# SSD mixer of a two-layer diffusion backbone: both directions' decay factors from one masked exponent tile

## The chip, the core and the metric

The kernel runs on one core of a Trainium2 chip. TensorE (PE) multiplies matrices, VectorE (DVE) and ScalarE (ACT) do element-wise work, GpSimd (POOL) a smaller share of it, and SyncE's queue (SP) issues the DMAs. Each engine works through its own instructions in order and waits for the others by semaphores. The metric is the device time of one execution in microseconds.

## The reference, cut to what matters

Two layers act on 256 latent tokens and 256 context tokens of width 1024, float32 throughout. A layer is a SwiGLU half step, a token mixer and another SwiGLU half step. Layer 0's mixer is a bidirectional Mamba-2 SSD with 32 heads of 64 channels in 4 groups, state 128, and chunks of 128 tokens; layer 1's is a pooling mixer. The change lies in the SSD, in the part of a chunk that stays within the chunk:

```python
seg = a_cum[:, :, :, None] - a_cum[:, :, None, :]
mask = jnp.tril(jnp.ones((Q, Q), dtype=bool))[:, :, None, None]
Lmat = jnp.exp(jnp.where(mask, seg, -jnp.inf))
cb = jnp.einsum('bclgn,bcsgn->bclsg', Cc, Bc)
y_diag = jnp.einsum('bclsg,bclsge,bcsgep->bclgep', cb, Lmat, xdt)
...
y_lat = d_skip[:, None] * xl
for d in range(2):                       # d == 1 runs on flipped sequences
    ...
    y_lat = y_lat + flip(yl, d)
```

For a pair of tokens (s, t) the forward direction counts where s is not behind t, the backward direction where s is not ahead of t. The two meet only on the diagonal s = t, where the exponent is zero and the factor is the step dt of each direction. `d_skip` multiplies the token itself and is added once.

## The kernel before

The program is a straight line of instructions. A scheduler orders each engine's instructions from the program order by its own estimate of readiness, and semaphores are placed after that. So a change of the code in one place can move rows on every engine.

The first feed-forward part ends at about 404 us of the span, the mixer fills the time from its first projection at 412 us to about 713 us, and the other feed-forward parts and the pooling mixer follow. In the feed-forward parts and the projections each float32 weight tile arrives by DMA (`raw`), ACT rounds it to `hi` (L203), DVE, or POOL for some tiles, takes the rest `lo` (L208), and TensorE makes three products (L216 to L218). The weight tiles of the mixer live in a pool of four buffers.

The mixer works group by group, g = 0 to 3, eight heads each. The string `PLAN` sets the program order of its steps, one letter each: A projects and convolves (`ip`, `ca`, `xs`, and the transposes `ptr`), E makes the decay factors (`decays`), D multiplies them with the matrix C·B (`decays_cb`), Z makes the gate (`pz`), B makes the outputs (`stage_b`) and O the out-projection (`op`).

In E a DMA spreads one row of cumulated exponents per head over 128 partitions, into a tile `em` of 128 x 2048 per direction (L700). There are two `em` buffers in all, one for each direction. For even heads DVE clamps and shifts the exponents (L710) and ACT takes the exponential (L717). For odd heads ACT does the clamp as a Relu (L715) and the exponential (L719). In D TensorE forms C·B for both chunks (`pcb`), DVE masks it with one triangle per direction (L734), multiplies both directions' tiles by it (L742), and POOL adds the two (L743).

In B the states are made: DVE weights x (`x2`, L777 and L783), TensorE multiplies (`ph` L778, `p1` L785), ACT copies `h0` (L780), POOL scales it into `h1` (L787), and DVE adds `p1` to it (L788). POOL multiplies the token by the skip (L799), TensorE applies the summed factors (`py` L803) and the states (`po` L807). DVE adds the parts, and the gate, the norm and the transposes `pyt` (L833) end the group.

The two PSUM banks of tag "b" serve `ptr`, `pcb` and `pyt` here. POOL cannot run L787 before what stands ahead of it in its own order, and DVE not L777 of the second direction before L788 of the first.

Of the kernel before, what the change touches and what calls it, by code (L numbers as in the profile page):

```python
# [20 lines left out]
S = 256  # L21
NG = 4
HG = 8
# [13 lines left out]
C_DSK = C_ALOG + 64  # L37
# [29 lines left out]
def tile_hybrid_backbone(  # L67
# [19 lines left out]
    nc = tc.nc  # L87
    v, sc, pe, gp = nc.vector, nc.scalar, nc.tensor, nc.gpsimd
# [5 lines left out]
    small = ctx.enter_context(tc.tile_pool(name="small", bufs=4))  # L94
# [193 lines left out]
    ONE = slice(0, S)  # L288
# [301 lines left out]
    with ExitStack() as st:  # L590
        scp = st.enter_context(tc.tile_pool(name="scp", bufs=1))
# [53 lines left out]
        def bc8(ap):  # L645
            return ap.unsqueeze(2).to_broadcast([P, HG, HD])

        def h8(ap):
            return ap.rearrange("p (h x) -> p h x", x=HD)
# [43 lines left out]


        def decays(g, EM):
            for d in range(2):
                h0 = 32 * d + HG * g
                em = sd.tile([P, HG, 2, P], F32, tag="em", name="em")
                src = acd[h0 : h0 + HG, :].rearrange("h t -> (h t)").unsqueeze(0).to_broadcast([P, HG * S])
                nc.sync.dma_start(em.rearrange("p h j t -> p (h j t)"), src)  # L700
                EM.append(em)
            yield
            for d in range(2):
                for h in range(HG):
                    e = EM[d][:, h]
                    hc = 32 * d + HG * g + h

                    for j in range(2):
                        if h % 2 == 0:
                            v.tensor_scalar(  # L710
                                e[:, j, :], e[:, j, :], ac[:, 2 + j, hc : hc + 1], qs[:, j, hc : hc + 1],
                                op0=ALU.min, op1=ALU.add,
                            )
                        else:
                            sc.activation(e[:, j, :], e[:, j, :], AF.Relu, scale=-1.0, bias=ac[:, 2 + j, hc : hc + 1])  # L715
                    if h % 2:
                        sc.activation(EM[d][:, h - 1], EM[d][:, h - 1], AF.Exp)  # L717
                        for j in range(2):
                            sc.activation(e[:, j, :], e[:, j, :], AF.Exp, scale=-1.0, bias=ld[:, j, hc : hc + 1])  # L719
                        yield  # L720

        def decays_cb(g, A, EM):
            BT, CT = A["BT"], A["CT"]
            pcb = bank("pcb", "b")
            for j in range(2):
                pe.matmul(
                    pcb[:, j * P : (j + 1) * P], BT[:, S + j * P : S + (j + 1) * P], CT[:, j * P : (j + 1) * P],
                    start=True, stop=True,
                )
            cbs = []  # L730
            for d in range(2):
                cbm = XH[d][:, ONE].rearrange("p (j t) -> p j t", t=P)
                cbs.append(cbm)
                v.tensor_tensor(  # L734
                    cbm, pcb[:, 0:S].rearrange("p (j t) -> p j t", t=P),
                    tri[d].unsqueeze(1).to_broadcast([P, 2, P]), op=ALU.mult,
                )
            for j in range(2):
                for d in range(2):
                    cbm = cbs[d]  # L740
                    e = EM[d][:, :, j, :]
                    v.tensor_tensor(e, e, cbm[:, j, :].unsqueeze(1).to_broadcast([P, HG, P]), op=ALU.mult)  # L742
                gp.tensor_tensor(EM[0][:, :, j, :], EM[0][:, :, j, :], EM[1][:, :, j, :], op=ALU.add)  # L743
            yield


# [22 lines left out]
        def stage_b(g, A, EM, zs):  # L769
            CT, Bt, xt = A["CT"], A["Bt"], A["xt"]  # L770
            hin = []
            for d in range(2):
# [8 lines left out]
                j = 2 + d  # L781
# [14 lines left out]
            for j in range(2):  # L796
                xl = xt[:, 2 + j, :]
                y = sd.tile([P, 512], F32, tag="y", name="y")
                gp.tensor_tensor(h8(y), h8(xl), bc8(pk[:, C_DSK + HG * g : C_DSK + HG * g + HG]), op=ALU.mult)  # L799
                py = bank("py", "c")  # L800
                for h in range(HG):
                    hc = slice(h * HD, (h + 1) * HD)
                    pe.matmul(py[:, hc], EM[0][:, h, j, :], xl[:, hc], start=True, stop=True)  # L803
                v.tensor_tensor(y, y, py, op=ALU.add)
                for d in range(2):
                    po = bank("po", "c")
# [120 lines left out]
            v.tensor_tensor(w2[:, j, c], w2[:, j, c], to[:, k, c], op=ALU.add)  # L927
        sc.activation(w2, w2, AF.Exp)
        v.tensor_tensor(w2, w2, dtk, op=ALU.mult)
        eL = scp.tile([P, 64], F32, name="eL")  # L930
        for d in range(2):
            c = slice(32 * d, 32 * d + 32)
# [178 lines left out]
def _layout(inputs):  # L1111
# [32 lines left out]
    for g, w in enumerate((2, 4, 8, 16)):  # L1144
        def box(n):
# [11 lines left out]
            for l in range(2)  # L1157
# [11 lines left out]
    return {  # L1169
        "hx": np.concatenate([a["ctx"][0], a["x"][0]]),  # L1170
        "hxT": np.concatenate([a["ctx"][0].T, a["x"][0].T], axis=1),
                "pack": pack, "idn": np.eye(P, dtype=f), "tris": tris, "pmat": pmat, "gnorm": a["ssd_norm_g"].reshape(1, 2048),
        "ada": ada, "adan": adan, "wgu": wgu, "wd": wd, "win": win, "wz": wz,
        "wout": wout, "poolw": pw,
    }
# [20 lines left out]
```

## Time and profile before

| quantity | value |
|---|---|
| median of 3 runs | 1315.9 us (1314.4 to 1316.13) |
| profiled execution, its own time | 1308.84 us |
| span of that execution | 1307.1 us |
| PE busy over the span | 1248.1 us (95%) |
| DVE busy | 972.6 us (74%) |
| ACT busy | 596.7 us (46%) |
| POOL busy | 157.9 us (12%) |
| mean granted TensorE clock | 0.984 |

The profiled execution's own time is 1.7 us above its span. Shares over the whole span mix stages, so the views below are taken of the mixer, from 446 us (the end of the preparation of its exponents) to 713 us (the start of the last out-projection). In a timeline row the first number is the start, the second the time of the row's instructions together, and the brackets hold the engine's idle time before it and what released it.

### The profile page before, as it was taken

Reading aid. Unit: us, or ns where it says so; the run is one execution under the profiler, and the core shown is the slowest. Engines: PE = TensorE matmul, PEld = TensorE weight load, DVE = VectorE, ACT = ScalarE, POOL = GpSimd, SP = SyncE. Lnnn points to the kernel's source line nnn. Section 1 sums busy time; section 2 is a strip of 40 time slices with the busy share of each in tenths; the row PEclk is TensorE's granted clock in tenths of the full one; section 3 lists DMA queues with packets and bytes.
Section 4 is the critical chain, followed back from the end, with each engine's and each line's share of the span. In section 5 each row is a group of like instructions: output and inputs, shape, how many; then the busy total and the mean of one; then the engine's idle time right before and its main releaser. Section 6 shows DMA issues by size and latency. Waiting matters only on the chain.

```text
span 1307.1 us, 21106 instructions
## 1 busy us (share of the span) xinstructions
PE 1248.1 (95%) x8262; PEld 1110.3 (85%) x8262; DVE 972.6 (74%) x1545; ACT 596.7 (46%) x1023; POOL 157.9 (12%) x112
## 2 busy tenths in 40 slices
PE   5999999999999979999988999999999999999997
PEld 2688888888888757787776999999999999999997
DVE  3599988763367879988997998766978566965553
ACT  3342222222244766555453654544545446744441
POOL 1000000000003242434263300000200000200000
PEclk7999999999999989999999999999999999999999
DMA  9588888962223513434343599767689665375661
GB/s 351 185 312 278 270 314 310 312 226 86 76 93 105 176 52 123 160 115 146 134 148 118 194 326 323 263 207 243 240 311 314 184 207 189 106 240 194 181 184 33
DMA packets 74995, 262.45 MB, mean 201 GB/s; under 512 B 8272, under 2 KB 10768, under 8 KB 73872
## 3 DMA queue, kind: packets, MB, share of 16 engines
q1 hardware_dynamic: 74896, 261.11, 59.1%
q8 instruction: 65, 1.06, 0.3%
q14 instruction: 34, 0.28, 0.1%
HBM read 259.96 MB, written 1.11 MB: 200 GB/s over the span
## 4 chain that ended last, share of the span: by engine, by line
PE 76%; DVE 9%; DMA 5%; ACT 4%; issue 3%; POOL 3%; SPq 0%; POOLq 0%; DVEq 0%; ACTq 0%
PE gu L218 14%; PE gu L216 14%; PE gu L217 14%; PE dn L216 7%; PE dn L218 7%; PE dn L217 7%; DMA adaw<-in_ada_dram 4%; DVE lo L208 2%; DVE ca L630 1%; POOL em L743 1%; PE ip L218 1%; PE ip L217 1%; PE ip L216 1%; PE py L803 1%; PE po L807 1%
## 5 line engine op out<-in xcount | busy, mean ns | idle before, releaser
L208 DVE TENSOR_TENSOR lo<-raw,hi 128x1024 fp32r<-128x1024 f32 (+1 forms) x317 | 393.3, 1244 | 145.9 <-ACT hi L203 145.3
L203 ACT ACTIVATE hi<-raw 128x1024 fp32r<-128x1024 f32 (+1 forms) x333 | 342.0, 1037 | 299.9 <-PE dn L218 125.8
L216 PE MATMUL gu<-vh,hi 128*128 128x256 f32 (+1 forms) x1056 | 293.3, 278 | 4.5 <-DVE sg L1002 2.6
L218 PE MATMUL gu<-vl,hi 128*128 128x256 f32 (+1 forms) x1056 | 292.5, 277 | 0.2 <-DVE vl L991 0.2
L217 PE MATMUL gu<-vh,lo 128*128 128x256 f32 (+1 forms) x1056 | 292.6, 277 | 0.0
L145 DVE SCALAR_TENSOR_TENSOR junk<-adaw,cb 128x1024 bf16<-128x1024 f32 x152 | 183.9, 1222 | 43.9 <-DMA adaw<-in_ada_dram 43.2
L216 PE MATMUL dn<-hh,hi 128*128 128x256 f32 (+1 forms) x704 | 214.2, 304 | 0.0
L217 PE MATMUL dn<-hh,lo 128*128 128x256 f32 (+1 forms) x704 | 214.2, 304 | 0.0
L218 PE MATMUL dn<-hl,hi 128*128 128x256 f32 (+1 forms) x704 | 214.2, 304 | 0.0
L216 PEld LDWEIGHTS gu<-vh,hi 128*128 128x128 f32 x1056 | 198.7, 188 | 5.2 <-DVE sg L1002 2.8
L218 PEld LDWEIGHTS gu<-vl,hi 128*128 128x128 f32 x1056 | 198.4, 188 | 0.5 <-DVE vl L991 0.4
L217 PEld LDWEIGHTS gu<-vh,lo 128*128 128x128 f32 x1056 | 198.6, 188 | 0.0
L218 PEld LDWEIGHTS dn<-hl,hi 128*128 128x128 f32 x704 | 132.1, 188 | 6.9
L217 PEld LDWEIGHTS dn<-hh,lo 128*128 128x128 f32 x704 | 132.1, 188 | 6.9
L216 PE MATMUL gu<-uh,hi 128*128 128x512 f32 x352 | 138.0, 392 | 0.0
L216 PEld LDWEIGHTS dn<-hh,hi 128*128 128x128 f32 x704 | 132.1, 188 | 6.8
L218 PE MATMUL gu<-ul,hi 128*128 128x512 f32 x352 | 137.9, 392 | 0.0
L217 PE MATMUL gu<-uh,lo 128*128 128x512 f32 x352 | 137.4, 390 | 0.0
L257 POOL TENSOR_TENSOR rs<-ms,mhalf 128x2 f32<-128x2 f32 (+1 forms) x6 | 5.4, 906 | 934.4 <-DVE ms L255 934.4
L307 ACT ACTIVATE hh<-hf 128x256 fp32r<-128x256 f32 (+1 forms) x88 | 40.9, 465 | 91.5 <-DVE hf L338 90.0
L336 ACT ACTIVATE sg<-gu 128x256 f32<-128x256 f32 (+1 forms) x79 | 34.7, 439 | 98.2 <-PE gu L218 98.2
L218 PEld LDWEIGHTS gu<-ul,hi 128*128 128x128 f32 x352 | 66.2, 188 | 15.2 <-issue 0.8
(264 smaller groups left out, 1883.6 us busy)
## 6 DMA issues: line engine op xcount, KB each, us to landing
raw<-in_wgu_dram SPq DMA_DIRECT2D x176, 512.0 KB, 4.6
adaw<-in_ada_dram SPq DMA_DIRECT2D x128, 512.0 KB, 5.0
raw<-in_wd_dram SPq DMA_DIRECT2D x64, 512.0 KB, 3.7
raw<-in_win_dram SPq DMA_DIRECT2D x25, 512.0 KB, 3.4
raw<-in_wd_dram SPq DMA_DIRECT2D x32, 384.0 KB, 3.6
adan<-in_adan_dram SPq DMA_DIRECT2D x16, 512.0 KB, 8.4
raw<-in_wz_dram SPq DMA_DIRECT2D x16, 512.0 KB, 3.7
em<-acd SPq DMA_DIRECT2D x8, 1024.0 KB, 4.8
```

What stands on the lines that cost most here:

```text
L145: v.scalar_tensor_tensor(junk, w, 1.0, cb2[i], op0=ALU.mult, op1=ALU.mult, accum_out=M[l][:, t, i : i + 1])
L203: sc.activation(hi[:, 0:n], r[:, 0:n], AF.Copy)
L208: (sub or v).tensor_tensor(lo[:, 0:n], r[:, 0:n], f32(hi[:, 0:n]), op=ALU.subtract)
L216: pe.matmul(out, wh, xh, start=start, stop=False)
L217: pe.matmul(out, wl, xh, start=False, stop=False)
L218: pe.matmul(out, wh, xl, start=False, stop=stop)
L307: sc.activation(a, h, AF.Copy)
L336: sc.activation(sg, pg, AF.Silu)
L630: v.scalar_tensor_tensor(avw[:, :, lo:hi], ov[:, :, lo + off : hi + off], hw[:, 5 * t + k : 5 * t + k + 1], avw[:, :, lo:hi], op0=ALU.mult ...
L743: gp.tensor_tensor(EM[0][:, :, j, :], EM[0][:, :, j, :], EM[1][:, :, j, :], op=ALU.add)
L803: pe.matmul(py[:, hc], EM[0][:, h, j, :], xl[:, hc], start=True, stop=True)
L807: pe.matmul(po, CT[:, j * P : (j + 1) * P], hin[d][0 if j == d else 1], start=True, stop=True)
```

## The change

Both directions now share one exponent tile. E loads the backward exponents first (`back`), then the forward ones (`e`). ACT shifts the backward ones by the difference `qd` of the two directions' per-token terms, as 16 Identity activations with a bias. A TensorE transpose of a strictly upper triangle (`above`) puts the mask for s behind t into a PSUM bank of tag "b" (`pmk`). DVE copies the masked backward exponents into the forward tile with two predicated copies. ACT then takes the exponential of that one tile with the forward bias, 16 activations of 128 x 128. The clamps go away, since no masked-out place is raised to a power any more.

In D, ACT copies C·B out of PSUM once. DVE multiplies the one tile by it, two instructions of 128 x 1024 where there were four, and POOL's sum is gone. The diagonal of the one tile carries the forward share only, so DVE reads the diagonal of C·B with an accumulating instruction and forms `co` = dt(backward) · diagonal + skip. L799's product takes `co` in place of the skip. `qd` and `above` are made once.

```diff
         def decays(g, EM):
-            for d in range(2):
-                h0 = 32 * d + HG * g
+            for d in (1, 0):
                 em = sd.tile([P, HG, 2, P], F32, tag="em", name="em")
...
+            back, e = EM
             yield
-                        if h % 2 == 0:
-                            v.tensor_scalar(
-                                e[:, j, :], e[:, j, :], ac[:, 2 + j, hc : hc + 1], qs[:, j, hc : hc + 1],
-                                op0=ALU.min, op1=ALU.add,
-                            )
-                        else:
-                            sc.activation(e[:, j, :], e[:, j, :], AF.Relu, scale=-1.0, bias=ac[:, 2 + j, hc : hc + 1])
-                    if h % 2:
-                        sc.activation(EM[d][:, h - 1], EM[d][:, h - 1], AF.Exp)
-                        for j in range(2):
-                            sc.activation(e[:, j, :], e[:, j, :], AF.Exp, scale=-1.0, bias=ld[:, j, hc : hc + 1])
-                        yield
+            for h in range(HG):
+                for j in range(2):
+                    sc.activation(
+                        back[:, h, j, :], back[:, h, j, :], AF.Identity, bias=qd[:, j, hcs[h] : hcs[h] + 1]
+                    )
+                if h % 2 and h < HG - 1:
+                    yield
+            pm = bank("pmk", "b")
+            pe.transpose(pm[:, 0:P], above, ident)
+            below = pm[:, 0:P].bitcast(mybir.dt.int32).unsqueeze(1).to_broadcast([P, HG, P])
+            for j in range(2):
+                v.copy_predicated(e[:, :, j, :], below, back[:, :, j, :])
+            yield
+            for h in range(HG):
+                for j in range(2):
+                    sc.activation(e[:, h, j, :], e[:, h, j, :], AF.Exp, bias=qs[:, j, hcs[h] : hcs[h] + 1])
+                if h % 2:
+                    yield
...
-            for d in range(2):
-                cbm = XH[d][:, ONE].rearrange("p (j t) -> p j t", t=P)
...
+            cb = XH[0][:, ONE]
+            sc.activation(cb, pcb[:, 0:S], AF.Copy)
...
-                gp.tensor_tensor(EM[0][:, :, j, :], EM[0][:, :, j, :], EM[1][:, :, j, :], op=ALU.add)
+                v.scalar_tensor_tensor(
+                    tmp("jd", "a", P), cj, 1.0, ident, op0=ALU.mult, op1=ALU.mult, accum_out=dg[:, j : j + 1]
+                )
+                v.scalar_tensor_tensor(
+                    co[:, j, :], dtk[:, 2 + j, 32 + HG * g : 32 + HG * g + HG], dg[:, j : j + 1],
+                    pk[:, C_DSK + HG * g : C_DSK + HG * g + HG], op0=ALU.mult, op1=ALU.add,
+                )
+                e = EM[1][:, :, j, :]
+                v.tensor_tensor(e, e, cj.unsqueeze(1).to_broadcast([P, HG, P]), op=ALU.mult)
...
-                gp.tensor_tensor(h8(y), h8(xl), bc8(pk[:, C_DSK + HG * g : C_DSK + HG * g + HG]), op=ALU.mult)
+                gp.tensor_tensor(h8(y), h8(xl), bc8(A["co"][:, j, :]), op=ALU.mult)
```

The change moves rows as well. On PE, at the first group's states and factors, before (`uh` and `ul` are the tokens, `x` under `ph` the weighted tokens `x2`):

```order
L755 MATMUL pz<-hi,uh_3282 128x512 x2
L642 MATMUL ptr<-cs,xs 128x128 x4
L778 MATMUL ph<-x_3877,Bt 128x512
L778 MATMUL ph<-x_3880,Bt 128x512
L785 MATMUL p_3887<-x_3885,Bt 128x512
L778 MATMUL ph<-x_3893,Bt 128x512
L778 MATMUL ph<-x_3896,Bt 128x512
L785 MATMUL p_3903<-x_3901,Bt 128x512
L803 MATMUL py<-xt,em 128x64 x8
```

and after:

```order
L783 MATMUL ph<-x_3864,Bt 128x512
L783 MATMUL ph<-x_3867,Bt 128x512
L218 MATMUL ip<-ul_3295,hi 128x512
L790 MATMUL p_3874<-x_3872,Bt 128x512
L216 MATMUL ip<-uh_3288,hi 128x512
L217 MATMUL ip<-uh_3288,lo 128x512
L783 MATMUL ph<-x_3880,Bt 128x512
L783 MATMUL ph<-x_3883,Bt 128x512
L218 MATMUL ip<-ul_3296,hi 128x512
L216 MATMUL ip<-uh_3289,hi 128x512
L217 MATMUL ip<-uh_3289,lo 128x512
L790 MATMUL p_3890<-x_3888,Bt 128x512
```

Before, the six state products stood in one block right after a transpose. Now 16 more projection products of the mixer stand ahead of them, and six stand between them.

On DVE, at the end of the second group's outputs, where the third group's factors are made, before:

```order
L804 TENSOR_TENSOR y<-y,py 128x512
L810 TENSOR_TENSOR yo<-po,ea 128x512
L821 TENSOR_SCALAR rs_4682<-rs_4680 128x1
L208 TENSOR_TENSOR lo<-raw,hi 128x1024
L824 SCALAR_TENSOR_TENSOR y<-y,rs_4682,x_85 128x256
L824 SCALAR_TENSOR_TENSOR y<-y,rs_4682,x_86 128x256
L811 TENSOR_TENSOR y<-y,yo 128x512
L810 TENSOR_TENSOR yo<-po,ea 128x512
L710 TENSOR_SCALAR em<-em,ac,qs 128x128 x4
```

and after:

```order
L809 TENSOR_TENSOR y<-y,py 128x512
L829 SCALAR_TENSOR_TENSOR y<-y,rs_4643,x_85 128x256
L829 SCALAR_TENSOR_TENSOR y<-y,rs_4643,x_86 128x256
L815 TENSOR_TENSOR yo<-po,ea 128x512 x2
L816 TENSOR_TENSOR y<-y,yo 128x512 x2
L716 COPY_PREDICATED em<-pmk,em 128x8x128 x2
L826 TENSOR_SCALAR rs_4727<-rs_4725 128x1
L829 SCALAR_TENSOR_TENSOR y<-y,rs_4727,x_85 128x256
L829 SCALAR_TENSOR_TENSOR y<-y,rs_4727,x_86 128x256
```

The two predicated copies, which read both tiles of exponents, now stand six instructions behind the last use of `py` (the `x2` rows count twice); the tile of forward exponents that they read is loaded into the buffer that this `py` has just released.

## Rows read from the trace of the kernel before

**Rows 1.** Windows of the whole mixer: columns, and the sum over four windows.

```profile
core 0: us, PE busy (x) PEld busy (x) DVE busy (x) ACT busy (x) POOL busy (x), PEclk, DMA share, GB/s
sum 267.00, PE 244.50 PEld 193.07 DVE 241.06 ACT 153.05 POOL 101.44; mean PE 61.12 PEld 48.27 DVE 60.27 ACT 38.26 POOL 25.36
```

**Rows 2.** Timeline of PE: start, time, row, idle before it and its releaser.

```profile
471.53 0.73 PE L755 MATMUL pz<-hi,uh 128*128 128x512 f32 x2 [0.85 <-ACT hi L203]
474.49 3.68 PE L778 MATMUL ph<-x,Bt 128*128 128x512 f32 x4 [1.80 <-DVE x L777]
479.39 1.10 PE L778 MATMUL ph<-x,Bt 128*128 128x512 f32 x2 [0.35 <-DVE x L777]
484.83 2.07 PE L778 MATMUL ph<-x,Bt 128*128 128x512 f32 x2 [4.34 <-DVE x L777]
...
523.54 0.63 PE L642 MATMUL ptr<-cs,xs 128*128 128x128 f32 x4 [1.66 <-DVE xs L636]
...
542.76 1.00 PE L642 MATMUL ptr<-cs,xs 128*128 128x128 f32 x4 [2.02 <-DVE xs L636]
...
669.32 0.63 PE L642 MATMUL ptr<-cs,xs 128*128 128x128 f32 x4 [0.85 <-DVE xs L636]
...
683.33 1.12 PE L642 MATMUL ptr<-cs,xs 128*128 128x128 f32 x4 [3.70 <-DVE xs L636]
```

**Rows 3.** Timeline of POOL, and of DVE (last row), at the first group's states.

```profile
471.04 6.20 POOL L743 TENSOR_TENSOR em<-em 128x1024 f32<-128x1024 f32 x1 [33.04 <-DVE em L742]
...
480.11 2.33 POOL L743 TENSOR_TENSOR em<-em 128x1024 f32<-128x1024 f32 x1
482.41 1.04 POOL L787 TENSOR_TENSOR h<-h,eL 128x512 f32<-128x512 f32 x1
...
483.48 0.69 DVE L788 TENSOR_TENSOR h<-h,p 128x512 f32<-128x512 f32 x1 [4.23 <-POOL h L787]
```

**Rows 4.** Windows of PE around its waits: length, busy time, granted clock, DMA.

```profile
475.00:481.00 6.00, 5.14 (x8) 0.75 0.00 0
485.00:491.00 6.00, 6.00 (x23) 0.73 0.50 180
543.00:549.00 6.00, 6.00 (x28) 0.73 0.51 195
683.00:689.00 6.00, 5.67 (x24) 0.73 0.77 285
...
525.00:530.00 5.00, 5.00 (x24) 1.00 0.57 191
```

**Rows 5.** Groups of the mixer by form: count, busy us and mean ns.

```profile
L710 DVE TENSOR_SCALAR em<-em,ac,qs 128x128 f32<-128x128 f32 x64 | 23.1, 409 | 0.1
L742 DVE TENSOR_TENSOR em<-em,x 128x1024 f32<-128x1024 f32 x16 | 18.9, 1214 | 0.0
L734 DVE TENSOR_TENSOR x<-pcb,cs 128x256 f32<-128x256 f32 x8 | 3.3, 410 | 0.0
L743 POOL TENSOR_TENSOR em<-em 128x1024 f32<-128x1024 f32 x8 | 31.2, 3912 | 56.7 <-DVE em L742 56.7
L715 ACT ACTIVATE em<-em,ac 128x128 f32<-128x128 f32 x64 | 22.1, 392 | 6.7 <-DMA em<-acd 6.7
L717 ACT ACTIVATE em<-em 128x256 f32<-128x256 f32 x32 | 12.8, 409 | 7.7 <-DVE em L710 7.6
```

**Rows 6.** DMA issues on the page: KB each, median us to landing.

```profile
em<-acd SPq DMA_DIRECT2D x8, 1024.0 KB, 4.8
```

**Rows 7.** Timelines of DVE (two rows) and POOL (last) where both subtract or multiply.

```profile
471.48 2.35 DVE L742 TENSOR_TENSOR em<-em,x 128x1024 f32<-128x1024 f32 x2
...
519.45 3.35 DVE L208 TENSOR_TENSOR lo<-raw,hi 128x1024 fp32r<-128x1024 f32 x1
...
519.30 2.42 POOL L208 TENSOR_TENSOR lo<-raw,hi 128x1024 fp32r<-128x1024 f32 x1 [6.65 <-ACT hi L203]
```

More of the change, by code (lines that the diff above doesn't have):

```diff
@@ L695, in decays @@
         def decays(g, EM):
-            for d in range(2):
-                h0 = 32 * d + HG * g
+            hcs = [HG * g + h for h in range(HG)]
+            for d in (1, 0):
                 em = sd.tile([P, HG, 2, P], F32, tag="em", name="em")
-                src = acd[h0 : h0 + HG, :].rearrange("h t -> (h t)").unsqueeze(0).to_broadcast([P, HG * S])
-                nc.sync.dma_start(em.rearrange("p h j t -> p (h j t)"), src)
+                src = acd[32 * d + HG * g : 32 * d + HG * g + HG, :].rearrange("h t -> (h t)")
+                nc.sync.dma_start(em.rearrange("p h j t -> p (h j t)"), src.unsqueeze(0).to_broadcast([P, HG * S]))
@@ L729, in decays_cb @@
                 )
-            cbs = []
-            for d in range(2):
-                cbm = XH[d][:, ONE].rearrange("p (j t) -> p j t", t=P)
[L733 to L736, printed above, removed]
-                )
[L738 to L742, printed above, removed]
-                gp.tensor_tensor(EM[0][:, :, j, :], EM[0][:, :, j, :], EM[1][:, :, j, :], op=ALU.add)
+            cb = XH[0][:, ONE]
+            sc.activation(cb, pcb[:, 0:S], AF.Copy)
+            dg = small.tile([P, 2], F32, tag="dg", name="dg")
+            co = small.tile([P, 2, HG], F32, tag="co", name="co")
+            A["co"] = co
+            for j in range(2):
+                cj = cb[:, j * P : (j + 1) * P]
+                v.scalar_tensor_tensor(
+                    tmp("jd", "a", P), cj, 1.0, ident, op0=ALU.mult, op1=ALU.mult, accum_out=dg[:, j : j + 1]
+                )
+                v.scalar_tensor_tensor(
[4 more added lines that the diff above has]
+                v.tensor_tensor(e, e, cj.unsqueeze(1).to_broadcast([P, HG, P]), op=ALU.mult)
             yield
@@ L802, in stage_b @@
                     hc = slice(h * HD, (h + 1) * HD)
-                    pe.matmul(py[:, hc], EM[0][:, h, j, :], xl[:, hc], start=True, stop=True)
+                    pe.matmul(py[:, hc], EM[1][:, h, j, :], xl[:, hc], start=True, stop=True)
                 v.tensor_tensor(y, y, py, op=ALU.add)
@@ L929, in tile_hybrid_backbone @@
         v.tensor_tensor(w2, w2, dtk, op=ALU.mult)
+        qd = scp.tile([P, 2, 32], F32, name="qd")
+        v.tensor_tensor(qd, qs[:, :, 32:64], qs[:, :, 0:32], op=ALU.subtract)
+        above = scp.tile([P, P], F32, name="above")
+        v.tensor_tensor(above, tri[0], ident, op=ALU.subtract)
         eL = scp.tile([P, 64], F32, name="eL")
@@ L1171, in _layout @@
         "hxT": np.concatenate([a["ctx"][0].T, a["x"][0].T], axis=1),
-                "pack": pack, "idn": np.eye(P, dtype=f), "tris": tris, "pmat": pmat, "gnorm": a["ssd_norm_g"].reshape(1, 2048),
+        "pack": pack, "idn": np.eye(P, dtype=f), "tris": tris, "pmat": pmat, "gnorm": a["ssd_norm_g"].reshape(1, 2048),
         "ada": ada, "adan": adan, "wgu": wgu, "wd": wd, "win": win, "wz": wz,
```

4 lines of the change are left out of this document (removed).

## The prediction, written before the result was known

> **What bounds the kernel now.** I read the page's list of engines first: TensorE is busy for 95% of the span, so only its idle time and its slow time can be won. I then took the windows of the mixer, the only stage that the change touches. From 446 to 713 us TensorE is busy for 244.5 of 267 us, so 22.5 us are idle; DVE is busy for 241.1 us, nearly as long, and ACT for only 153 [rows 1]. So here DVE is a second bound, and the next question is who ends TensorE's waits. The timeline of PE answers it: the eight waits shown are ended by DVE in all but one case, and add up to 15.6 us: 0.85 + 1.80 + 0.35 + 4.34 = 7.3 in the first group, and 1.66 + 2.02 + 0.85 + 3.70 = 8.2 later [rows 2]. The other 6.9 us are shorter waits and the chain that ends the last group, which the change leaves alone.
>
> The longest of them, 4.34 us, has a chain that can be followed. POOL adds the two directions' tiles, one for 6.20 us, the other until 482.4; only then can it scale the state (L787), which stands behind both in its order. DVE sits idle for 4.23 us until that is done, and its next products come too late for TensorE [rows 2, 3].
>
> Idle time costs a second time. After the waits of 1.80, 4.34, 2.02 and 3.70 us the granted clock has a spell at its lower level, 1.2 instead of 2.4 GHz. In the four windows it averages 0.75 or 0.73 while TensorE is almost fully busy, a loss of (1 - 0.75) x 6 = 1.5 us once and (1 - 0.73) x 6 = 1.6 us three times. After the wait of 1.66 us the clock stayed at 1.00 [rows 2, 4]. Two spells belong to the first group (3.1 us), two to the later ones (3.2 us).
>
> **The change part by part.** *POOL.* Eight sums go, 31.2 us [rows 5]. In the first group nothing is left on POOL ahead of L787 but the two products with `co`, so its release is the copy of the state by ACT. What is late next there? Four times TensorE alternates with one DVE product of 128x512 (for `ph`, `p1`, `ph`, `p1`), and a DVE instruction of that shape takes 0.69 us [rows 3]. I leave these four, 2.8 us, as waits, and count 7.3 - 2.8 = **4.6 us** as gone. The moved order helps: 16 projection products now stand ahead of the block and six inside it, so TensorE has work while DVE makes the factors. In pieces of 0.7 us the idle time is well below the 1.66 us after which the clock held, so I count both spells as gone, **3.1 us** [rows 2, 4].
>
> *DVE.* Removed: L710 with 23.1 us, L734 with 3.3, and eight of the sixteen L742 at 1.214, which is 9.7; together 36.1 us [rows 5]. Added: eight predicated copies of 128x1024, which the trace doesn't show. From below they cost what L742 costs for the same number of elements, 1.214, since no instruction of this size in those rows is cheaper; from above I take twice that, 2.43, should reading a mask, a source and a destination need two passes. That gives 9.7 to 19.4 us. I take 9.7, since L742 also reads two tiles and writes one. Sixteen small instructions for the diagonal and `co` and two for the preparation are each smaller than L734's 128x256, 0.410, so 7.4 us at most and, at about half, 4 us. Net, DVE loses 36.1 - 9.7 - 4 = 22.4 us, 5.6 us for each group, and at the worst prices 9.3 us. The four later waits of 8.2 us all end with `xs`, the convolution's output on DVE, which queues there among these very instructions but also among the weight subtractions, which stay. So I let half of it go, **4.1 us**, and one of the two later spells, **1.6 us** [rows 2, 4].
>
> *ACT.* 64 Relu at 0.392 (25.1 us), as many exponentials of that shape at L719, and 32 of 128x256 at 0.409 (13.1) go; 64 Identity and 64 Exp of that same shape come, and four copies of 128x256. Net that is 13.1 less four times about 0.4, some 11 us won on an engine that is idle for 114 of 267 us. I count nothing for it: its slack hides it either way [rows 1, 5].
>
> *PE.* Four transposes more, one per group. Four of the same shape take 0.63 us in one row, so four cost **0.6 us** [rows 2]. They hold one of two "b" banks until the copies are done. In the order of after the next two users of such banks stand far enough behind them, so I count nothing; if a transpose `ptr` had to wait for it, it would be the DVE wait of the next part.
>
> *The new wait.* In the third and fourth groups the forward exponents land in the buffer that the group before has just released by its last `py`. The load takes 4.8 us [rows 6]. On DVE the copies stand six instructions behind the use of that `py`: four of 128x512 at 0.69 and two half as large, some 3.5 us. So DVE will stand still for about 1.3 us in each of these groups, and behind it queue the norm's scaling, the next convolution and the next weight split. TensorE has 18 projection and 48 gate products in that place in the third group; at 24 in 5.00 us [rows 4] that is 13.8 us of cover. I count **1.0 us** for both groups together. The issues on SP gain from the change: the backward tile's buffer is free after the copies rather than after POOL's sum, so a load that stands behind it in SP's order starts no later. No bytes are added, and I count nothing.
>
> **The sum.** -4.6 - 3.1 - 4.1 - 1.6 + 0.6 + 1.0 = -11.8 us. Against the profiled execution's own time (span 1307.1 plus 1.7 around it) that is 1308.8 - 11.8 = 1297.0. The median of the runs shown, 1315.9, lies 7.1 us above that execution; the difference is carried over as it is: 1315.9 - 11.8 = **1304.1 us**.
>
> **The rivals.** (E) *More than that.* All eight waits and four spells go: 15.6 + 6.3 - 0.6 = 21.3 us, so 1294.6. For it speaks that POOL also delays DVE directly: a subtraction on DVE took 3.35 us while POOL ran one of 2.42 beside it. Against it: two L742 took only 2.35 us together, their normal pace, while POOL was at its sum, and it was POOL that took 6.20 instead of 2.33 [rows 3, 7].
>
> The Trainium skill, "GPSIMD Engine Reference", section "Key points", says that GpSimd shares its SBUF interfaces with VectorE and contends with VectorE instructions that have two SBUF inputs. By that rule the sum would move towards E, since 31 us of such sharing go. The trace agrees only in part: the subtraction of 3.35 us obeys it, and the two multiplications of 2.35 us don't show it on DVE's side.
>
> (A) *A chain takes the place of the sum.* Before, even and odd heads ran on DVE and ACT side by side. Now 16 Identity (6.3), two copies (2.4), 16 Exp (6.3) and two multiplications (2.4) follow each other, 17.4 us, with ACT's weight rounding in between [rows 5]. If the first group's factors are no earlier for that, TensorE waits at `py` instead, and the first group's 7.7 us stay: 1315.9 - 4.1 = 1311.8. Against it: POOL's 8.5 us at the end of the old chain are longer than what the new one adds.
>
> (B) *No difference.* POOL, free earlier, runs its own subtractions earlier, and these collide with DVE's as at 519 us [rows 7]. Then the later 5.7 us don't come, and half of the first group's goes: -3.9 + 1.6 = -2.3, so 1313.6. Against it: the number of POOL's subtractions is the same.
>
> (C) *Slower.* The copies stop DVE, in the third and fourth groups, for the load's 4.8 us and 2 x 2.43 of their own, some 9.7 us, with all of `lo` and `xs` behind them. That decides once DVE's backlog exceeds TensorE's 13.8 us of cover, so if 4 us of backlog stood there already. Beyond it each further us is TensorE's; with 4.5 us of wait and a spell of 1.6 in each group it costs 12.2, the later gain of 5.7 is lost, and the first group's 7.7 are won: 12.2 - 7.7 + 0.6 = +5.1, so 1321.0. Against it: at the low price DVE has 5.6 us less to do per group.
>
> **How the numbers follow.** A measurement of this kernel can tell about 0.2%, 2.6 us, from no change. I give the forecast (6 to 18 us faster) 58%, E 8%, A 14%, B 11%, C 9%. Faster by over 0.2%: 58 + 8 + 14 = 80%; within it, B with 11%; slower, C with 9%. The range runs from 1294 (E's end) to 1315 (B's end with its scatter) and leaves out C and a little of B and E.
>
> **What would show it.** Right: no POOL row holds the state's scaling in the first group, the wait of 4.34 us before `ph` is gone, and no window there has a clock below 0.9; the predicated copies take about 1.2 us; DVE's busy time falls by some 22 us and POOL's by some 31; the end of the mixer moves ahead by some 12 us and all later parts keep their lengths. Wrong: a wait of TensorE at `py`, or at `ptr` behind a predicated copy, of more than 2 us, copies of over 2 us, or DVE idle on the load of `em` for more than 3 us at a time.

## The result and the profile after

The changed kernel takes 1308.5 us (median of 13 runs, 1304.1 to 1310.1), the kernel before 1315.1 us in its 13 runs beside them. The ratio is 0.9945, with a 95% interval of 0.9926 to 0.9964, so it is 0.55% faster; the two medians lie 6.6 us apart. The forecast was 11.8 us. The profiled execution of after has 1306.04 us and a span of 1304.3 us.

First I cut both spans at the two ends of the mixer. The view by tile gives, for each line, the count, the shortest, middle and longest duration in ns, and the first and last start. Of before, the mixer's first projection and the first product behind the mixer:

```profile
L216 PE MATMUL ip<-uh,hi x184: 278/389/803, 412.2 to 666.8; 128*128 128x512 f32 x168, 128*128 128x256 f32 x16
...
L216 PE MATMUL gu<-vh,hi x204: 276/276/389, 726.7 to 799.9; 128*128 128x256 f32 x78, 128*128 128x258 f32 x24
```

The same two rows of after:

```profile
L216 PE MATMUL ip<-uh,hi x184: 279/393/797, 419.0 to 664.4; 128*128 128x512 f32 x168, 128*128 128x256 f32 x16
...
L216 PE MATMUL gu<-vh,hi x217: 276/276/385, 722.5 to 799.9; 128*128 128x256 f32 x85, 128*128 128x258 f32 x24
```

The mixer now starts 6.8 us later (419.0 against 412.2) and lasts 303.5 us instead of 314.5. So it gained 11.0 us, near the forecast, and the feed-forward part in front of it, whose code and instruction order the change leaves alone, lost 6.8. The part behind it lasts 581.8 against 580.4 us.

Windows of exactly these two stretches answer to [rows 1], with the same columns. Before:

```profile
412.20:726.70 314.50, 288.13 (x1484) 228.86 (x1482) 275.40 (x429) 181.49 (x374) 119.43 (x70) 0.97 0.38 129
```

After:

```profile
419.00:722.50 303.50, 286.45 (x1488) 223.78 (x1486) 260.87 (x382) 173.27 (x346) 88.29 (x62) 1.00 0.39 134
```

TensorE's idle time went from 314.5 - 288.1 = 26.4 us to 303.5 - 286.5 = 17.0, and its granted clock from a mean of 0.97 to 1.00. DVE is busy for 14.5 us less, POOL for 31.1.

The timeline of PE in after, the first group's waits and the longer ones behind it, answers to [rows 2] (`ph` is L783 now, `p` L790, `pyt` L838):

```profile
480.65 0.66 PE L642 MATMUL ptr<-cs,xs 128*128 128x128 f32 x4 [0.59 <-DVE xs L636]
...
483.74 1.13 PE L783 MATMUL ph<-x,Bt 128*128 128x512 f32 x2 [0.56 <-DVE x L782]
...
485.19 1.12 PE L783 MATMUL ph<-x,Bt 128*128 128x512 f32 x2 [0.32 <-DVE x L782]
...
489.15 1.12 PE L783 MATMUL ph<-x,Bt 128*128 128x512 f32 x2 [0.26 <-DVE x L782]
...
630.58 1.12 PE L790 MATMUL p<-x,Bt 128*128 128x512 f32 x2 [1.76 <-DVE x L788]
...
666.51 0.39 PE L216 MATMUL op<-yh,hi 128*128 128x256 f32 x1 [1.26 <-DVE ca L630]
...
684.85 1.12 PE L790 MATMUL p<-x,Bt 128*128 128x512 f32 x2 [1.63 <-DVE x L788]
```

In the first group 0.59 + 0.56 + 0.32 + 0.26 = 1.7 us are left of 7.3. None of the later waits is longer than 1.8 us. The view of the waits from 446 to 714 us adds them up:

```profile
PE p L790 <- DVE x L788: 3.9, 3, 1.8
...
PE ptr L642 <- DVE xs L636: 2.0, 3, 1.2
```

At the transposes `ptr` 2.0 us are left of the 8.2 us that the later part of [rows 2] holds, so more went there than the forecast's half. But 3.9 us of waits at `p` are new, all ended by L788 on DVE. POOL's timeline at the first group's states answers to [rows 3]:

```profile
476.28 2.41 POOL L208 TENSOR_TENSOR lo<-raw,hi 128x1024 fp32r<-128x1024 f32 x1 [31.58 <-ACT hi L203]
482.02 2.57 POOL L804 TENSOR_TENSOR y<-xt,co 128x512 f32<-128x512 f32 x2 [3.32 <-DMA raw<-in_wz_dram]
487.03 1.52 POOL L792 TENSOR_TENSOR h<-h,eL 128x512 f32<-128x512 f32 x1 [2.44 <-ACT h L785]
```

Windows of PE at this place answer to [rows 4] (length, busy time, granted clock, DMA):

```profile
480.00:486.00 6.00, 4.52 (x18) 1.00 0.21 80
486.00:492.00 6.00, 5.71 (x16) 1.00 0.00 0
```

No spell of the lower clock follows these waits. The scaling of the state (L792 now) is released by ACT's copy, no longer by POOL's own backlog. Groups of the mixer in after, by form, answer to [rows 5]:

```profile
L208 DVE TENSOR_TENSOR lo<-raw,hi 128x1024 fp32r<-128x1024 f32 x42 | 57.3, 1372 | 3.7 <-ACT hi L203 3.5
...
L716 DVE COPY_PREDICATED em<-pmk,em 128x1024 f32<-128x1024 int32 x8 | 10.7, 1347 | 0.2 <-PE pmk L713 0.2
...
L788 DVE TENSOR_TENSOR x<-xt,w 128x512 f32<-128x512 f32 x8 | 9.2, 1152 | 0.0
...
L740 DVE SCALAR_TENSOR_TENSOR jd<-x,cs 128x128 f32<-128x128 f32 x8 | 5.6, 697 | 0.0
...
L743 DVE SCALAR_TENSOR_TENSOR co<-dtk,dg,pk 128x8 f32<-128x8 f32 x8 | 2.6, 326 | 0.0
```

A predicated copy takes 1.347 us, close to the lower bound. The subtractions L208 on DVE took 66.6 us for the same 42 in before.

### The profile page after: what moved, and what is told of

Same layout as the page of the kernel before. It is cut to its first block, busy times and chain, and to the rows that moved or that the text cites. A ratio compares the mean times of both kernels' runs of the same rounds, so it can differ in the third digit from the quotient of the medians.

```text
span 1304.3 us, 21043 instructions
## 1 busy us (share of the span) xinstructions
PE 1256.3 (96%) x8266; PEld 1108.2 (85%) x8266; DVE 957.8 (73%) x1499; ACT 588.6 (45%) x995; POOL 126.0 (10%) x104
## 3 DMA queue, kind: packets, MB, share of 16 engines
HBM read 259.96 MB, written 1.11 MB: 200 GB/s over the span
## 4 chain that ended last, share of the span: by engine, by line
PE 78%; DVE 9%; DMA 6%; ACT 3%; issue 2%; POOL 1%; SPq 0%; POOLq 0%; DVEq 0%; ACTq 0%
PE gu L218 14%; PE gu L216 14%; PE gu L217 13%; PE dn L216 7%; PE dn L218 7%; PE dn L217 7%; DMA adaw<-in_ada_dram 4%; DVE lo L208 2%; DVE ca L630 2%; PE ip L216 1%; PE ip L218 1%; PE ip L217 1%; PE py L808 1%; PE po L812 1%; PE op L218 1%
## 5 line engine op out<-in xcount | busy, mean ns | idle before, releaser
L208 DVE TENSOR_TENSOR lo<-raw,hi 128x1024 fp32r<-128x1024 f32 (+1 forms) x317 | 384.0, 1215 | 145.3 <-ACT hi L203 144.3
L216 PEld LDWEIGHTS gu<-uh,hi 128*128 128x128 f32 x352 | 66.5, 189 | 15.2 <-ACT uh L499 0.4
```

Source lines behind the costliest of these rows:

```text
L208: (sub or v).tensor_tensor(lo[:, 0:n], r[:, 0:n], f32(hi[:, 0:n]), op=ALU.subtract)
L216: pe.matmul(out, wh, xh, start=start, stop=False)
```

## The experiments

Two theories were on the table for each half. Of the mixer's gain: POOL's sum stood in the chain of the states (the prediction's), or DVE's load was the bound. Of the loss ahead of it: the two new small tiles, which move every later tile by 384 bytes within a partition, or scatter between executions. The table gives, for each profiled execution, the start of the mixer, its length, what follows, and the span, in us; the ratios go by several runs. The last three kernels ran once each.

| kernel | start | mixer | behind | span | ratio to before |
|---|---|---|---|---|---|
| before | 412.2 | 314.5 | 580.4 | 1307.1 | |
| before_again | 413.9 | 316.0 | 580.9 | 1310.8 | 1.0014 [0.9979, 1.0049] |
| before_shifted | 420.2 | 317.6 | 580.1 | 1317.9 | 1.0033 [1.0010, 1.0055] |
| before_dve_sum | 412.4 | 320.1 | 579.8 | 1312.3 | 1.0052 [1.0028, 1.0076] |
| after | 419.0 | 303.5 | 581.8 | 1304.3 | 0.9945 [0.9926, 0.9964] |
| after_again | 418.3 | 305.9 | 581.5 | 1305.7 | 0.9944 [0.9919, 0.9968] |
| after_realigned | 412.8 | 305.6 | 586.5 | 1304.9 | 0.9912 [0.9881, 0.9944] |
| after_low | 414.1 | 305.5 | 584.4 | 1304.0 | 0.9921 [0.9897, 0.9946] |
| after_low_again | 412.2 | 305.7 | 583.1 | 1301.0 | 0.9916 [0.9882, 0.9949] |
| low_pool_sum | 413.2 | 318.8 | 580.5 | 1312.5 | 1.0017 [0.9988, 1.0046] |
| low_copies_twice | 412.3 | 314.9 | 579.2 | 1306.4 | 0.9988 [0.9963, 1.0014] |
| after_pad64 | 420.7 | 305.5 | 580.2 | 1306.4 | |
| after_pad192 | 415.5 | 308.7 | 580.4 | 1304.6 | |
| after_wpad | 419.4 | 304.2 | 582.4 | 1306.0 | |

**The two kernels once more.** No edit.

> The kernel before, unchanged, once more. Theory 'execution' (the first feed-forward part, which the change leaves alone, differs from one execution to the next, and the 6.8 us by which the mixer begins later in the trace of after, 419.0 against 412.2 us, are chance): the mixer begins anywhere between 410 and 420 us here. Theory 'address' (two small new tiles move every later tile by 384 bytes, and TensorE reads the moved tokens more slowly): it begins at 412 us again, within 1.5 us, with its 128x512 matrix products of the first part at a mean of 389 ns. Ratio to the kernel before 1.000 by both.

> The changed kernel, unchanged, once more. Theory 'execution': the mixer begins anywhere between 410 and 420 us. Theory 'address': it begins at 419 us again, within 1.5 us, with the 128x512 products of the first part at a mean of 392 to 393 ns. From there to the first product of the next part 303.5 us by both, within 2 us. Ratio 0.9945 by both.

Both the later start and the shorter mixer return: 413.9 to 418.3 and 316.0 to 305.9. Two of the bounds were drawn too tight: the start of before_again lies 1.7 us and not 1.5 from 412.2, and the mixer of after_again 2.4 us and not 2 from 303.5. Over both pairs the mixer gains 10.6 us in the mean and the start loses 5.6.

**The tiles put back.** The kernel has padding tiles ahead of its large pools. Raising two of them completes the shift to 512 bytes:

```diff
-    skip(upool[0], 128)
+    skip(upool[0], 256)
...
-    skip(wp1, 128)
+    skip(wp1, 256)
```

> The changed kernel with 128 bytes more of padding ahead of the token tiles and of the later weight buffers, so that these tiles stand 512 bytes and not 384 behind their places before. The order of every engine is the same as in the changed kernel. Theory 'address': the products of the first part are back at 389 ns, the mixer begins at 412 us, and the time is 6 to 8 us under the changed kernel's, so about 1301 us where before is 1315 (ratio 0.989 to 0.991). Theory 'execution': nothing changes, ratio 0.9945 within its interval.

And the kernel before, shifted by 384 bytes with nothing else changed:

```diff
-    skip(upool[0], 128)
+    skip(upool[0], 512)
...
-    skip(wp1, 128)
+    skip(wp1, 512)
```

> The kernel before with 384 bytes more of padding in the same two places, and nothing else; its orders are the same as before. Theory 'address': the products of the first part take 392 to 393 ns, the mixer begins at 419 us, and the time is 6 to 9 us above before (ratio 1.005 to 1.007). Theory 'execution': ratio 1.000 within 0.002.

The start follows the shift both ways: 412.8 with the tiles put back, 420.2 with the old kernel shifted. The gate's products in before_shifted, by the view by tile, have a middle duration of 392 ns instead of before's 389, with the same instructions in the same order:

```profile
L216 PE MATMUL gu<-uh,hi x352: 389/392/776, 28.1 to 378.1; 128*128 128x512 f32 x176
```

So the loss is the place of the tiles, and not the new work. The ratio of after_realigned, 0.9912, just misses its range, since what follows the mixer takes 586.5 us there. The price in the whole time of before_shifted, 0.33% or 4.3 us, is smaller than expected.

**The two small tiles elsewhere.** They go to the mixer's own pool, which is laid behind the first part's tiles:

```diff
-            dg = small.tile([P, 2], F32, tag="dg", name="dg")
-            co = small.tile([P, 2, HG], F32, tag="co", name="co")
+            dg = scp.tile([P, 2], F32, tag="dg", name="dg", bufs=4)
+            co = scp.tile([P, 2, HG], F32, tag="co", name="co", bufs=4)
```

> The changed kernel with its two new small tiles (the diagonal and the skip's factor) in the mixer's own pool, so that every tile ahead of that pool and every tile of the later parts stands at the same address as before the change; all orders are those of the changed kernel. Theory 'address': the mixer begins at 412 to 414 us as in the kernel before, it takes 302 to 306 us, the rest 580 to 582 us, and the ratio to before is 0.986 to 0.990, 5 to 8 us under the changed kernel's. Rival (only the padding of the realigned kernel happened to help, and what it lost in the last part is part of it): the start is at 418 us and the ratio 0.994.

> The same program as the version with the two small tiles in the mixer's own pool, to see whether the slower stretch behind the mixer in its one profile (584.4 us against 580 before) belongs to the program or to that execution. If to the execution: the part behind the mixer takes 579 to 582 us, ratio 0.990 to 0.994. If to the program: 583 to 586 again. Mixer 303 to 307 us in both.

The start is back at 414.1 and 412.2, the mixer keeps its gain. With 1303.8 us and 1301.4 us, against 1312.9 and 1310.1 us of before on the same chips, this version is 0.8% faster than before. The changed kernel's ratio is 0.9945; the intervals of the two overlap, so that this version is the faster of them is likely and not shown. The expected 0.986 to 0.990 was not reached: what follows takes 583 to 584 us instead of 580. There, with no wait, the products of the second projection run slower from about 810 to 900 us. Groups of PE from 840 to 880 us in before:

```profile
L216 PE MATMUL dn<-hh,hi 128*128 128x256 f32 x87 | 24.0, 276 | 0.0
```

and in after_low_again:

```profile
L216 PE MATMUL dn<-hh,hi 128*128 128x256 f32 x106 | 29.8, 281 | 0.0
```

In the repeat it came in the same place, so it belongs to this program or its timing, as the second expectation there says. It is not the addresses alone: low_copies_twice has its tiles at the same places and doesn't show it. after_realigned shows such a stretch from 1120 us to the end. Its cause stays open.

**Which tile's place it is.** Three more paddings on the changed kernel. In before, the tokens `uh` and `ul`, two of the six weight buffers and the hidden tiles of the first feed-forward all lie at 448 bytes modulo 512, in after at 320. The other four weight buffers lie ahead of the small tiles and move in none of these kernels.

```diff
-    skip(upool[0], 128)
+    skip(upool[0], 192)
```

> The changed kernel with the padding ahead of the token tiles raised from 128 to 192 bytes, so that tokens, weight tiles and hidden tiles of the first feed-forward stand 448 bytes behind the place they had before the change, modulo 512 at 384 where they stood at 448 before and at 320 in the changed kernel. If only the place of before is fast (any other residue is slow), its products take 392 to 394 ns in the mean and the mixer's first projection starts at 418 to 420 us. If the granularity is coarser and the changed kernel's 320 alone is bad, they take 389 to 391 ns and it starts at 412 to 414 us.

```diff
-    skip(upool[0], 128)
+    skip(upool[0], 320)
```

> The same with the padding at 320 bytes: the tiles stand at 0 modulo 512. If only the place of before is fast: 392 to 394 ns, start at 418 to 420 us. If tiles that begin on a round address are as good or better: 389 ns or less, start at 412 to 414 us or before it.

```diff
         wp0 = st.enter_context(tc.tile_pool(name="wp0", bufs=2))
+        skip(wp0, 128)
```

> The changed kernel with 128 bytes of padding in the pool of the first feed-forward's weight tiles, behind the tokens: the tokens stay at the changed kernel's shifted place, the weight tiles (and the hidden tiles that are laid behind them) go back to their residue of before. If the place of the tokens, which stream through TensorE, sets the pace: gate products stay at 394 to 397 ns by line, the second projection's products, which stream hidden tiles, fall back to 389. If the place of the weights sets it: both go back to 389 to 392 and the mixer starts at 412 to 414 us. If it is neither but the distance of the two: gate products differ from both, and the start lies elsewhere.

The view by tile of the first feed-forward's products tells them apart by the middle of the three durations. Before (448), the gate's and the second projection's:

```profile
L216 PE MATMUL gu<-uh,hi x352: 389/389/775, 26.9 to 370.9; 128*128 128x512 f32 x176
...
L216 PE MATMUL dn<-hh,hi x112: 389/389/389, 273.6 to 403.5; 128*128 128x512 f32 x112
```

After (320):

```profile
L216 PE MATMUL gu<-uh,hi x352: 389/392/776, 27.1 to 376.9; 128*128 128x512 f32 x176
...
L216 PE MATMUL dn<-hh,hi x112: 387/392/404, 277.9 to 410.2; 128*128 128x512 f32 x112
```

after_wpad, tokens at 320 and the weight and hidden tiles at 448:

```profile
L216 PE MATMUL gu<-uh,hi x352: 390/393/776, 26.9 to 378.0; 128*128 128x512 f32 x176
...
L216 PE MATMUL dn<-hh,hi x112: 389/389/393, 279.2 to 410.7; 128*128 128x512 f32 x112
```

after_pad192, all at 0:

```profile
L216 PE MATMUL gu<-uh,hi x352: 388/392/776, 28.0 to 374.0; 128*128 128x512 f32 x176
L217 PE MATMUL gu<-uh,lo x352: 388/394/628, 28.6 to 374.2; 128*128 128x512 f32 x176
L218 PE MATMUL gu<-ul,hi x352: 388/388/796, 30.1 to 374.4; 128*128 128x512 f32 x176
```

With after_wpad the gate's products, which stream tokens, stay at 393 ns although their weights are back, and the second projection's, which stream hidden tiles, return to 389. So for the gate's products the place of the streamed tile sets the pace, not that of the weights. The mixer's projection says the same: it streams the moved tokens with weights from the four buffers that don't move, and its middle duration goes from 389 to 393 ns in the first two views of the section on the result. For the second projection, hidden and weight tiles went back together, so there it is not separated. after_pad64 (384) is slow, with 393 ns and the start at 420.7. At 0 it is mixed: the products with `ul` are as fast as ever, those with `uh` slow, and the start is between, at 415.5. So neither of the two rules that I had written down holds, and what property of the place counts stays open. The pace follows from counts: windows from 100 to 160 us hold 266 products in before and 262 in after. 60 us / 262 - 60 us / 266 = 3.4 ns, and 1584 products of the first part (352 and 176 on each of three lines) make 5.4 us.

**POOL's sums put back.** after_low, with the old sum behind each multiplication. It goes into the backward tile, which nothing reads any more, so it is extra work and no value changes:

```diff
                 v.tensor_tensor(e, e, cj.unsqueeze(1).to_broadcast([P, HG, P]), op=ALU.mult)
+                gp.tensor_tensor(EM[0][:, :, j, :], EM[0][:, :, j, :], EM[1][:, :, j, :], op=ALU.add)
```

> As after_low, but POOL does the old sum of two tiles of 128x1024 again, eight in all, into a tile that nothing needs; the scheduler places them ahead of the scaling of the state, as before. Theory 'POOL's place in the chain' (the sum held up the state's scaling and so TensorE): the waits of TensorE at the first group's states rise from 1.7 us to 5 us or more, the clock falls there, and the mixer takes 4 to 9 us more than in after_low. Rival 'DVE's load' (the gain came from DVE's 22 us alone): the mixer is longer by less than 2 us.

It cost more than I had expected: the mixer takes 318.8 us, 13.3 more than after_low's, and the whole gain is gone. Waits of 2.64 and 0.77 us return at the first states, less than the 5 us expected, but also 3.18 and 2.95 us at later transposes:

```profile
480.11 1.97 PE L784 MATMUL ph<-x,Bt 128*128 128x512 f32 x2 [2.64 <-DVE x L783]
...
537.87 0.77 PE L642 MATMUL ptr<-cs,xs 128*128 128x128 f32 x4 [3.18 <-DVE xs L636]
...
672.36 1.11 PE L642 MATMUL ptr<-cs,xs 128*128 128x128 f32 x4 [2.95 <-DVE xs L636]
```

The granted clock falls behind them, to 0.52 from 480 to 486 us and to 0.50 from 672 to 678. Windows of the mixer, after_low:

```profile
414.10:719.60 305.50, 286.66 (x1489) 226.10 (x1487) 260.56 (x382) 173.30 (x346) 88.38 (x62) 0.99 0.39 133
```

and low_pool_sum:

```profile
413.20:732.00 318.80, 293.12 (x1489) 231.25 (x1487) 271.32 (x382) 173.90 (x346) 112.61 (x70) 0.96 0.37 128
```

Of the 13.3 us, 6.8 are idle time of TensorE (25.7 against 18.8) and 6.5 are busy time, with the clock at 0.96 in the mean. DVE has 382 instructions in both, but they take 271.3 us instead of 260.6: POOL's sums cost DVE 10.8 us by running beside it. By form, 10.2 of these fall on the small new instructions for the diagonal, which the kernel before doesn't have. In after_low `jd` takes 5.2 us and `co` 2.6, in low_pool_sum:

```profile
L740 DVE SCALAR_TENSOR_TENSOR jd<-x,cs 128x128 f32<-128x128 f32 x8 | 9.1, 1140 | 0.0
L743 DVE SCALAR_TENSOR_TENSOR co<-dtk,dg,pk 128x8 f32<-128x8 f32 x8 | 8.9, 1113 | 0.0
```

So the 10.8 us are not what the old sums cost DVE in before. DVE's timeline in low_pool_sum shows the first ones:

```profile
474.84 2.34 DVE L743 SCALAR_TENSOR_TENSOR co<-dtk,dg,pk 128x8 f32<-128x8 f32 x1
...
479.38 3.42 DVE L783 TENSOR_TENSOR x<-xt,w 128x512 f32<-128x512 f32 x2
```

and POOL's what ran beside them:

```profile
474.39 2.77 POOL L749 TENSOR_TENSOR em<-em 128x1024 f32<-128x1024 f32 x1 [1.37 <-DVE em L748]
...
479.39 2.86 POOL L749 TENSOR_TENSOR em<-em 128x1024 f32<-128x1024 f32 x1
...
485.64 1.04 POOL L793 TENSOR_TENSOR h<-h,eL 128x512 f32<-128x512 f32 x1 [1.94 <-ACT h L786]
```

An instruction on 128x8 that ends in 0.22 us elsewhere took 2.34, until the sum was done. The last row answers the theory on trial: POOL stood idle for 1.94 us before it scaled the state, and ACT's copy released it. So the sums did not hold up the scaling here, and the wait of 2.64 us is DVE's weighting of x (L783), slowed beside the second sum. The old chain was not put back by this run.

**DVE's load.** after_low, with each predicated copy issued twice (the second copies the same values):

```diff
-                v.copy_predicated(e[:, :, j, :], below, back[:, :, j, :])
+                for _ in range(2):
+                    v.copy_predicated(e[:, :, j, :], below, back[:, :, j, :])
```

> As after_low, but each predicated copy is done twice over, which adds 8 x 1.3 = 10.8 us to DVE, 2.7 us in each group, and changes no value. Theory 'half of DVE's relief reaches the end' (the prediction's term): the mixer is 3 to 7 us longer. Rival 'slack' (DVE's 22 us hardly mattered, the chain did): under 2 us longer. Rival C of the prediction (the copies stop DVE until TensorE has nothing left): over 8 us longer, with waits of TensorE in the third and fourth groups.

```profile
412.30:727.10 314.80, 289.38 (x1487) 228.55 (x1486) 271.75 (x390) 173.95 (x346) 88.17 (x62) 0.98 0.37 129
```

Eight copies more give 271.75 - 260.56 = 11.2 us on DVE, and the mixer takes 314.9 instead of 305.5 us: 9.4 us, more than the "half" that I had counted and in the range of rival C. By the medians of all runs it is 1311.5 - 1303.8 = 7.8 us. The timeline of PE shows the waits:

```profile
515.88 0.76 PE L216 MATMUL ip<-uh,hi 128*128 128x512 f32 x1 [3.81 <-DVE ca L630]
...
536.39 0.66 PE L642 MATMUL ptr<-cs,xs 128*128 128x128 f32 x4 [1.69 <-DVE xs L636]
...
662.24 0.94 PE L642 MATMUL ptr<-cs,xs 128*128 128x128 f32 x4 [2.77 <-DVE xs L636]
```

The first two follow the copies of the second group, not of the third, where rival C had put them. And this is not the load alone, since the edit moved rows too. In after_low twelve gate products stand ahead of the projection's last rows in the second group, up to 516.91 us, and TensorE doesn't wait there. The first of them:

```profile
514.19 0.39 PE L760 MATMUL pz<-hi,uh 128*128 128x512 f32 x1
```

In low_copies_twice gate products stand among the first group's states already, and none stands in the 3.81 us:

```profile
478.61 0.39 PE L761 MATMUL pz<-hi,uh 128*128 128x512 f32 x1
```

So up to 516.91 - 514.19 = 2.7 us of cover left that place by the order. The edits of low_pool_sum and before_dve_sum move rows of TensorE and DVE as well. What DVE's time costs by itself was not measured.

**The sum on DVE.** The kernel before, with its sum moved off POOL, to take the sum out of POOL's order without the rest of the change:

```diff
-                gp.tensor_tensor(EM[0][:, :, j, :], EM[0][:, :, j, :], EM[1][:, :, j, :], op=ALU.add)
+                v.tensor_tensor(EM[0][:, :, j, :], EM[0][:, :, j, :], EM[1][:, :, j, :], op=ALU.add)
```

> The kernel before with its eight sums on DVE in place of POOL, nothing else. Theory 'POOL's place in the chain': the wait of 4.34 us before the state products shrinks to under 2 us though DVE has 9.7 us more to do; the mixer is 1 to 6 us shorter than 314.5 to 316. Rival 'DVE's load': DVE is the bound, so the mixer is 3 us or more longer.

The wait of 4.34 us that POOL's order made is down to 1.11, but the wait ahead of it is now 2.93 instead of 1.80 us, and the kernel is 0.52% slower:

```profile
476.21 3.81 PE L778 MATMUL ph<-x,Bt 128*128 128x512 f32 x4 [2.93 <-DVE x L777]
...
483.15 1.13 PE L778 MATMUL ph<-x,Bt 128*128 128x512 f32 x2 [1.11 <-DVE x L777]
```

The window of its mixer:

```profile
412.40:732.50 320.10, 288.56 (x1485) 226.12 (x1483) 285.25 (x437) 181.93 (x375) 93.03 (x62) 0.98 0.37 127
```

DVE's time in the mixer rises by 9.8 us (285.2 against 275.4) and the mixer by 5.6. This execution is the fastest of its ten, 1314.0 us against a median of 1321.8, so the 5.6 us are rather too little. The chain is a local truth; in the total, what the sums cost on DVE, together with the moved rows, was more.

## Why the prediction was half right

The direction was right and the time lay in the range, but the gain was about half of the forecast. **The step that failed** is the last sentence of "Right": "all later parts keep their lengths", and with it the unspoken one that the earlier part keeps its own. The sum had no term for the place of the tiles. I had looked for the cost of the two small tiles `dg` and `co` in their instructions, not in the 384 bytes by which they, with four buffers each, push everything behind them. This term is worth 5.6 us in the two pairs of profiles, about the difference between 11.8 and 6.6. That it matches so well is partly chance: the two pairs of spans differ by only 2.8 and 5.1 us, since the part behind the mixer is 1.0 us longer in the mean, and the medians rest on many executions of which no profile was kept.

Point by point, from the profiles of before and after:

| step of the sum | forecast | measured |
|---|---|---|
| waits of the first group | -4.6 | -5.6 (7.3 to 1.7) |
| other idle time of the mixer: later waits -4.1, new wait +1.0 | -3.1 | -3.7 (idle 26.4 to 17.0, less the line above) |
| clock spells -3.1 and -1.6, transposes +0.6: TensorE's busy time | -4.1 | -1.7 (288.1 to 286.5) |
| the mixer | -11.8 | -11.0 |
| ahead of it and behind it | 0 | +6.8 and +1.4 |

*The first group* went as told: POOL's row no longer holds the scaling, the 4.34 us are gone, and no window of 6 us from 450 us to the mixer's end has a clock below 0.95. *The clock* did better than counted in this execution, with no spell left instead of one, yet TensorE's busy time fell less than counted. The slower stream explains part: 504 of the mixer's projection products (168 on each of three lines) also stream the shifted tokens, and 504 x 3.4 ns = 1.7 us. The spells vary: after_again has one window of 0.73, after_low one of 0.73 and, later, two of 0.92 and 0.79.

*The new wait* is not there. The copies waited for nothing but 0.2 us at `pmk`: the loads had landed, and DVE was at its other work until each copy began.

*DVE's relief* was 14.5 us instead of 22.4. The copies were priced well (10.7 against 9.7). Too cheap was the diagonal: with 5.6 + 2.6 us, and 0.6 for reading the accumulators, it takes 8.8 instead of 4, over the bound of 7.4 too. That bound went by size, and the trace shows why size is no bound: a `jd` that takes 0.28 us alone takes 1.49 beside a subtraction on POOL. Nor did I see that POOL's new place collides with DVE's weighting of x, which takes 24.4 us instead of 18.3: L782 has a mean of 0.977 us (0.771 as L777 in before) and L788 of 1.152 (0.764 as L783). Two L782 that take 2.13 us together, from 483.01, run beside the product of the token on POOL that is shown above (L804). Of the eight L788 six take 0.67 or 0.68 us; the other two, 2.71 from 627.81 and 2.44 from 682.36, run beside a weight subtraction on POOL, and the waits of 1.76 and 1.63 us at `p` follow them. On the other side, the subtractions L208 on DVE fell from 66.6 to 57.3 us, a gain that I had left to rival E. It is hardly the sums' going: in low_pool_sum, with sums, they take 58.8.

*How much of DVE's relief reaches TensorE* I had put at half of one set of waits. The transposes gave back more than half of theirs (6.2 of 8.2 us), and the new waits at `p` took 3.9 again. The runs that were to price it show only bundles: 11.2 us more on DVE came with 9.4 us more of mixer, and 10.8 us with 13.3, but with rows moved in both and one profile of each. That more than half passes on is likely and not shown.

*What POOL's order is worth* stays open too. The first group's 7.7 us (waits and spells) did go as told, and the rows show the chain before and its absence after. But low_pool_sum didn't restore the chain, and before_dve_sum, without a sum on POOL, has 9.8 us more on DVE and is slower. So no run separates the chain from DVE's load. That the mixer's 11.0 us agree with the forecast 11.8 is luck in part: DVE's relief was 7.9 us too small and TensorE's busy time fell by 2.4 us too little, while its waits fell by 9.3 us where 7.7 were counted.

The Trainium skill, "GPSIMD Engine Reference", section "Key points", says that GpSimd shares its interfaces to SBUF with VectorE and contends with its instructions that read two inputs there. The prediction found the trace to agree only in part. The runs agree more: 382 equal instructions take 10.8 us more beside the sums, 10.2 of them on `jd` and `co`, which both read two tiles in SBUF. What the two rows of [rows 7] on L742 showed, a multiplication not slowed, is one case.

Of the rivals, *E* had a right mechanism in the collisions, but POOL's products with `co` and its subtractions brought part of them back on L782 and L788. *B*'s collisions are those two slow L788; its time was wrong because on L208 they became fewer, not more. *A*'s chain doesn't show: no wait of TensorE at `py`. *C* didn't happen; whether its premise holds, that DVE's time passes on to TensorE in full once the cover is used up, no run shows by itself.

## What to carry to other kernels

When a change adds even a tiny tile, look at which tiles move: compare the duration of untouched instructions in untouched stages first, before explaining anything in the changed one. Here it was enough to put the new small tiles into a pool that is laid behind the tokens. When two engines are both nearly full in a stage, price the second one's time by a run that adds a known amount to it (here, a copy issued twice), and compare the orders of both programs before reading the price: here they had changed. Count an instruction's price beside the other engine's work, not by its size alone.

## What the runs showed that was not expected

The place of a streamed tile in SBUF changes TensorE's pace: products of 128x512 go from 389 to 392 or 393 ns, and 266 to 262 of them in 60 us, when the tokens lie at 320 or 384 instead of 448 bytes modulo 512. Putting the two moved weight buffers back to their place changed nothing in the products that stream tokens.

A DVE instruction of 128x8 took 2.34 us instead of 0.22 when POOL added two tiles of 128x1024 at the same time. And in three executions, of two programs, TensorE ran whole stretches of 128x256 products, some 90 to 170 us long, at 281 instead of 276 ns at a granted clock of 1.00, without any wait; why is open.
